# One plain product of two units ahead of the first token sums; three additions for a weight sum, four pieces for a unit's finish

## The chip, the core and the metric

The kernel runs on one core of a Trainium2 chip. The metric is the device time of one execution in microseconds. The kernel was run three times: 2572.38 to 2576.52 us, median 2574.26 us. A separate, profiled execution left the trace from which all rows below are taken.

## The reference, cut to what matters

One decoder layer over 512 tokens of width 2048, batch 1, all in float32. What the change touches is the input projection, one matrix product whose columns are cut into heads, values and gates:

```python
mod = jnp.einsum('bd,de->be', jax.nn.silu(c), w_ada) + b_ada
shift, scale, gate = jnp.split(mod, 3, axis=-1)
u = rms_norm(x, norm_w) * (1.0 + scale[:, None]) + shift[:, None]
proj = jnp.einsum('bsd,de->bse', u, w_in)
(a_q, a_k, a_v, a_z, b_q, b_k, b_v, b_z,
 c_q, c_k, c_v, c_z, g_a, g_b, g_c) = jnp.split(proj, offsets, axis=-1)
...                       # three token mixers, SiLU gates, merge
y = jnp.einsum('bsd,de->bse', merged, w_out)
return x + gate[:, None] * y
```

`c_v`, the values of the dilated mixture, is 3072 columns wide: three of the units below.

## The kernel before, in words

**Precision.** Every float32 operand is split into a rounded high part and a remainder (`uh`, `ul` for the tokens; `xh`, `xl` for weights in this stage; `fh`, `fl` for sums of tokens), and one product takes three matmuls (`mm3`). For weights, ACT writes the high part (`xh`, a CAST of 128x2048) and DVE the remainder (`xl`, a subtraction of the same size): `x_split`.

**Units and jobs.** The stage here runs in the trace from about 221.75 us to about 1290 us. It multiplies 14 blocks of 1024 columns of `w_in` ("units") by a seven-product scheme on 2x2 blocks of tokens and weights. In the text u0, u1 and u2 are the three units of `c_v`; they are the first of the stage. A unit is a list of 14 jobs, each 24 matmuls of 128x512 (48 of 128x256 in the gate and query/key units):
- `P1` (2 jobs) and `P2` (2 jobs): plain products of a block of `u` with a block of weights (`pure_load`, `pure_mul`);
- `R3` (2 jobs): a plain block of weights times the token sum "2";
- 8 sum jobs: each loads four weight blocks, adds them up in place (`sum_load`) and feeds four products, `R6`, `R5`, `R7`, `Q4` (`sum_mul`).

P1, R3 end in `keep` (ACT copies the sum out of PSUM to the tiles `p1`, `r3`), P2 in `p2_done` (DVE adds `p1` to P2, tile `c`). The sum jobs end in `done_z` (DVE takes R6 out of PSUM, tile `z`), `done_s` (R5, tile `s`, then `r3 + s`) and `done_rest` (R7 twice, then Q4).

**PSUM.** There are two rotating groups of banks: `pj` with two, `at` with six. R6 always takes `pj`; R5, R7 and Q4 fill `at`. A product that takes a bank again waits until the engine that empties it has read it.

**The loop over jobs.** Its program order is the order on each engine. For job i: build a token sum if one is due; load job i+2 (with the additions of a sum job on DVE); split job i+1; split the token sum; multiply job i; then one finishing piece that is due, or all that are due when the job just done was the last of a plain product. The split weights have two buffers, so `xh` of job i+2 waits until PE has ended job i. The raw weights `xr` have three.

**Token sums.** `form_build` makes the eight sums of tokens that R3 and the sum jobs need: four DVE subtractions of 128x256 into a tile `d`, from rows of `u` that are read back from DRAM (`xr<-ud`, two DMAs on SP's queue, for every even build). They take a buffer of `xr` as weights do. `form_split` makes `fh` (ACT) and `fl` (DVE) of them. Builds take place in two of every three of the first 12 jobs: `form_build(i - i // 3) if i < 12 and i % 3 < 2`.

**Order of the first units.** `jobs = units[1][0] + units[2][0] + units[0][0] + units[0][1] + units[1][1] + units[2][1]`: P1 and P2 of u1, of u2 and of u0 come first (12 jobs), then R3 and sums of u0, of u1, of u2. For u1 and u2, `p1` waits in DRAM (`p1d`) until its unit's sums begin. From the fourth unit on, a unit runs P1, P2, R3, sums in one go.

Of the kernel before, what the change touches and what calls it, by code (L numbers as in the profile page):

```python
# [10 lines left out]
F32 = mybir.dt.float32  # L11
# [7 lines left out]
P = 128  # L19
# [8 lines left out]
A_Q, A_K, A_V, A_Z = 0, 1024, 2048, 3072  # L28
B_Q, B_K, B_V, B_Z = 4096, 4608, 5120, 6144
# [36 lines left out]
def hybrid_kernel(ctx, tc, x, c, w_in, w_pa, w_pb, w_pc, w_out, w_ada, b_ada, norm_w, lam,  # L66
                  da_w, ret_w, fin_w, k_ident, k_causal, k_band, k_tri4, k_sel, k_cos, k_sin,
                  k_decay, out):
    nc = tc.nc
# [30 lines left out]
    def pj():  # L100
        return psum.tile([P, 512], F32, tag="pj", name="pj", bufs=2)

    def at():
        return psum.tile([P, 512], F32, tag="at", name="at", bufs=6)
# [3 lines left out]
    graw_dram = dram.tile([KC, P, S], F32, tag="graw", name="graw")  # L108

    gate_of = {g: dram.tile([KC, P, S], F32, tag=f"g{g}", name=f"g{g}") for g in (G_A, G_B)}  # L110
    p1_dram = {u: dram.tile([P, 2, 512], F32, tag=f"p1d{u}", name=f"p1d{u}") for u in (3, 4)}
    part_dram = dram.tile([KC, P, S], F32, tag="part", name="part")
    u_dram = dram.tile([KC, P, S], F32, tag="ud", name="ud")

# [420 lines left out]
    def block_mul(pss, name, j, h, l, fm):  # L535

        if fm:
            b = tokens(name, j, slice(0, 256))
            for cb in range(4):
                cs = slice(cb * P, (cb + 1) * P)  # L540
                o = pss[cb // 2][:, (cb % 2) * 256:(cb % 2) * 256 + 256]
                mm3(o, h[:, cs], l[:, cs], *b, j == 0 and cb % 2 == 0, j == HJ - 1 and cb % 2 == 1)
        else:
            for q in range(2):
                mm3(pss[q], *tokens(name, j, slice(q * P, (q + 1) * P)), h, l, j == 0, j == HJ - 1)

    def unit_jobs(w, c0, put, fm=False, early=None):


        st = {}  # L550

        def pure_load(k0, cc):
            r = wxp.tile([P, 4, 512], F32, tag="xr", name="xr", bufs=3)
            sync.dma_start(out=r, in_=w[k0:k0 + 512, cc:cc + 512].rearrange("(j p) c -> p j c", p=P))
            return r

        def pure_mul(key, name, t, hl):
            if t == 0:
                st[key] = [pj() if key == "P1" or (early is not None and key == "R3") else at() for _ in range(2)]
            for jj in range(4):  # L560
                block_mul(st[key], name, 4 * t + jj, hl[0][:, jj, :], hl[1][:, jj, :], fm)

        def keep(key, tag):
            t = evp.tile([P, 2, 512], F32, tag=tag, name=tag)
            for q in range(2):
                act.copy(t[:, q, :], st[key][q])
            st[tag] = t

        def p2_done():
            t = evp.tile([P, 2, 512], F32, tag="c", name="c")  # L570
            for q in range(2):
                dve.tensor_add(t[:, q, :], st["p1"][:, q, :], st["P2"][q])
            put(t, 0, 0)
            if early is not None:
                nc.gpsimd.dma_start(out=early, in_=st["p1"])

        def sum_load(j):
            r = wxp.tile([P, 4, 512], F32, tag="xr", name="xr", bufs=3)
            for i in range(2):
                sync.dma_start(out=r[:, 2 * i:2 * i + 2, :],  # L580
                                     in_=w[(i * HJ + j) * P:(i * HJ + j + 1) * P, c0:c0 + 1024]
                                     .rearrange("p (a c) -> p a c", a=2))
            for o, a in ((0, 1), (1, 3), (3, 0), (2, 3)):
                dve.tensor_add(r[:, o, :], r[:, o, :], r[:, a, :])
            return r

        def sum_mul(j, hl):
            if j == 0:
                st["R6"] = [pj() for _ in range(2)]
                for key in ("R5", "R7", "Q4"):  # L590
                    st[key] = [at() for _ in range(2)]
                if early is not None:
                    st["p1"] = evp.tile([P, 2, 512], F32, tag="p1", name="p1")
                    nc.gpsimd.dma_start(out=st["p1"], in_=early)
            for key, name, o in (("R6", "1", 3), ("R5", "0", 0), ("R7", "3", 1), ("Q4", "A22", 2)):
                block_mul(st[key], name, j, hl[0][:, o, :], hl[1][:, o, :], fm)


        def done_z():
            z = st["z"] = evp.tile([P, 2, 512], F32, tag="z", name="z")  # L600
            for q in range(2):
                dve.tensor_sub(z[:, q, :], st["R6"][q], st["p1"][:, q, :])

        def done_s():
            z, r3 = st["z"], st["r3"]
            s = st["s"] = evp.tile([P, 2, 512], F32, tag="s", name="s")
            for q in range(2):
                dve.tensor_add(s[:, q, :], z[:, q, :], st["R5"][q])
            dve.tensor_add(r3, r3, s)
            put(r3, 0, 512)  # L610

        def done_rest():
            z, s = st["z"], st["s"]
            for q in range(2):
                dve.tensor_add(z[:, q, :], z[:, q, :], st["R7"][q])
                dve.tensor_add(s[:, q, :], s[:, q, :], st["R7"][q])
            put(s, 1, 512)
            for q in range(2):
                dve.tensor_sub(z[:, q, :], st["Q4"][q], z[:, q, :])
            put(z, 1, 0)  # L620

        lists = []
        for key, name, k0, cc, done in (("P1", "A11", 0, 0, lambda: keep("P1", "p1")),
                                        ("P2", "A12", 1024, 0, p2_done),
                                        ("R3", "2", 1024, 512, lambda: keep("R3", "r3"))):
            lists.append([(lambda k0=k0, cc=cc, t=t: pure_load(k0 + t * 512, c0 + cc),
                           lambda hl, key=key, name=name, t=t: pure_mul(key, name, t, hl),
                           (done,) if t == HJ // 4 - 1 else ()) for t in range(HJ // 4)])
        lists.append([(lambda j=j: sum_load(j), lambda hl, j=j: sum_mul(j, hl),
                       (done_z, done_s, done_rest) if j == HJ - 1 else ()) for j in range(HJ)])  # L630
        return lists[0] + lists[1], lists[2] + lists[3]

    def put_values(unit):
        def put(t, half, cc):
            nc.gpsimd.dma_start(out=v_dram[unit][half * 256:half * 256 + 256, cc:cc + 512]
                                .rearrange("(q p) c -> p q c", p=P), in_=t)
        return put
# [4 lines left out]
    def put_gates(g, b0):  # L642
        def put(t, half, cc):
            def f():
                act.activation(out=t, in_=t, func=AF.Sigmoid)
                b = b0 + cc // P
                nc.gpsimd.dma_start(out=gate_of[g][b:b + 4, :, half * 256:half * 256 + 256]
                                    .rearrange("b p t -> p b t"), in_=t.rearrange("p q (a t) -> p (q a) t", a=2))
            deferred.append(f)
        return put  # L650
# [19 lines left out]
    def bias_add(n):  # L670
# [11 lines left out]
        if q == 7:  # L682
            nc.gpsimd.dma_start(out=br_dram[3 * g:3 * g + 3].rearrange("b p c -> p b c"),
                                in_=br.rearrange("p (b c) -> p b c", c=P))


    units = [unit_jobs(w_in, c0, put_values(unit), early=p1_dram.get(unit))
             for unit, c0 in ((2, C_V), (3, C_V + 1024), (4, C_V + 2048))]
    units += [unit_jobs(w_in, g + b0 * P, put_gates(g, b0), fm=True) for g in (G_A, G_B) for b0 in (0, 8)]
    units += [unit_jobs(w_in, c0, put_raw(dst), fm=True) for c0, dst in zip(QK, qk_dram)]  # L690
    units += [unit_jobs(w_in, c0, put_values(unit)) for unit, c0 in ((0, A_V), (1, B_V))]
    jobs = units[1][0] + units[2][0] + units[0][0] + units[0][1] + units[1][1] + units[2][1]
    for plain, summed in units[3:]:
        jobs += plain + summed
    raws = [jobs[0][0](), jobs[1][0]()]
    ready = x_split(raws.pop(0))
    for n, b in enumerate([NF - 1] + list(range(NF - 1))):
# [5 lines left out]
    later = []  # L703
    for i, (_, mul, done) in enumerate(jobs):

        sums = form_build(i - i // 3) if i < 12 and i % 3 < 2 else None
        due, deferred[:] = list(deferred), []
        if i + 2 < len(jobs):
            raws.append(jobs[i + 2][0]())
        nxt = x_split(raws.pop(0)) if raws else None  # L710
        if sums:
            form_split(*sums)
        for f in due:
            f()
        mul(ready)
        ready = nxt
        later += done
        for _ in range(len(later) if len(done) == 1 else min(1, len(later))):
            later.pop(0)()

        u, t = divmod(i, 14)
        if 4 <= u < 12 and t in (6, 8, 10):
            bias_load((u - 4) * 3 + (t - 6) // 2, ("z", "s", "c")[(t - 6) // 2])
        if 4 <= u < 12 and t in (8, 10, 12):
            bias_add((u - 4) * 3 + (t - 8) // 2)
# [1046 lines left out]
```

## Time and profile before

| | us |
|---|---|
| median of three runs (lowest, highest) | 2574.26 (2572.38, 2576.52) |
| the profiled execution, its own time | 2571.79 |
| span of its trace | 2570.0 |
| the first three units, 221.75 to 467.10 us | 245.35 |
| the other units, 467.10 to about 1290 us | 823 |

The span is what the trace covers; the execution's time is 1.8 us longer. PE is the engine that is busy nearly all the time, so a microsecond counts only where PE stands still, or runs at the lower of its two clock levels. The page of the profile gives busy times over the whole span; the views by stretch and of the single instructions show where PE stands.

### The profile page before, as it was taken

How to read it: one execution, taken by the hardware profiler on the slowest of the kernel's cores; microseconds unless marked ns; L12 is line 12 of the kernel's file. 1: busy time of each engine (PE TensorE's matmuls, PEld its weight loads, DVE VectorE, ACT ScalarE, POOL GpSimd, SP SyncE). 2: the span in 40 equal slices, each digit the busy share in tenths (PEclk: the TensorE clock that was granted, in tenths of full speed). 3: DMA queues.
4: the chain of work that ended last, by engine and by line, in shares of the span. 5: the costliest groups of instructions: out<-in, count | busy, mean ns of one | idle time of the engine just before them, and what ended most of it. 6: DMA issues, size and time to landing. Idle time of an engine off the chain costs nothing. (4 is left out here: it accounts for less than half of the span.)

```text
span 2570.0 us, 36726 instructions
## 1 busy us (share of the span) xinstructions
PE 2516.9 (98%) x14539; PEld 2224.0 (87%) x14539; DVE 1907.0 (74%) x2716; ACT 1134.4 (44%) x1476; POOL 179.9 (7%) x293
## 2 busy tenths in 40 slices
PE   7999999999999999999999999999999999999998
PEld 6787777999999999999887888888888888778888
DVE  7885888778887788877886777347887657786554
ACT  5233433443444333333336666346666436652223
POOL 0000000000000000000000001200000220003100
PEclk9999999999999999999999999999999999999999
DMA  9886765666666666666556555654333673439533
GB/s 346 294 293 233 253 213 213 218 209 212 234 233 228 220 209 231 236 223 231 208 183 198 153 160 146 198 162 118 109 113 107 191 222 98 118 113 297 190 133 113
DMA packets 363953, 504.83 MB, mean 196 GB/s; under 512 B 18850, under 2 KB 237748, under 8 KB 363396
## 3 DMA queue, kind: packets, MB, share of 16 engines
q1 hardware_dynamic: 329732, 401.89, 47.8%
q0 software_dynamic: 27136, 92.13, 10.4%
q10 hardware_dynamic: 6912, 8.46, 0.9%
q8 instruction: 114, 1.87, 0.3%
q14 instruction: 59, 0.48, 0.1%
HBM read 450.37 MB, written 52.04 MB: 195 GB/s over the span
## 5 line engine op out<-in xcount | busy, mean ns | idle before, releaser
L86 ACT CAST xh<-xr 128x2048 fp32r<-128x2048 f32 x196 | 374.3, 1910 | 589.7 <-PE at L86 478.8
L86 DVE TENSOR_TENSOR xl<-xr,xh 128x2048 fp32r<-128x2048 f32 x196 | 448.9, 2290 | 184.9 <-ACT xh L86 183.5
L86 DVE TENSOR_TENSOR wl<-wr,wh 128x1024 fp32r<-128x1024 f32 (+2 forms) x275 | 275.4, 1018 | 186.2 <-ACT wh L86 181.4
L86 PE MATMUL pj<-uh,wl 128*128 128x512 f32 x944 | 368.6, 390 | 3.6 <-DVE wl L86 3.6
L86 PE MATMUL pj<-uh,wh 128*128 128x512 f32 x944 | 371.8, 394 | 0.0
L86 ACT CAST wh<-wr 128x1024 fp32r<-128x1024 f32 (+2 forms) x275 | 239.3, 889 | 294.8 <-PE at L86 137.9
L86 PE MATMUL pj<-ul,wh 128*128 128x512 f32 x944 | 368.5, 390 | 0.0
L86 DVE TENSOR_TENSOR xr<-xr 128x512 f32<-128x512 f32 x448 | 309.3, 690 | 13.8 <-DMA xr<-in_w_in_dram 2.3
L86 PE MATMUL at<-fh,xl 128*128 128x256 f32 x864 | 244.9, 283 | 0.7 <-DVE xl L86 0.7
L86 PE MATMUL at<-fh,xh 128*128 128x256 f32 x864 | 244.5, 283 | 0.0
L86 PE MATMUL at<-fl,xh 128*128 128x256 f32 x864 | 244.5, 283 | 0.0
L86 PEld LDWEIGHTS pj<-uh,wl 128*128 128x128 f32 x944 | 177.7, 188 | 41.7 <-DVE wl L86 4.0
L86 PEld LDWEIGHTS pj<-ul,wh 128*128 128x128 f32 x944 | 177.9, 188 | 35.4
L86 PEld LDWEIGHTS pj<-uh,wh 128*128 128x128 f32 x944 | 177.7, 188 | 35.3
L86 PEld LDWEIGHTS at<-fh,xl 128*128 128x128 f32 x864 | 165.8, 192 | 0.9 <-DVE xl L86 0.9
L86 PEld LDWEIGHTS at<-fh,xh 128*128 128x128 f32 x864 | 165.8, 192 | 0.0
L86 PEld LDWEIGHTS at<-fl,xh 128*128 128x128 f32 x864 | 165.8, 192 | 0.0
L86 PE MATMUL at<-uh,xh 128*128 128x256 f32 x576 | 163.0, 283 | 0.0
L86 PE MATMUL at<-ul,xh 128*128 128x256 f32 x576 | 163.0, 283 | 0.0
L86 PE MATMUL at<-uh,xl 128*128 128x256 f32 x576 | 163.0, 283 | 0.0
L86 PE MATMUL at<-yh,wh 128*128 128x512 f32 x288 | 113.1, 393 | 2.2 <-ACT wh L86 2.2
L86 PE MATMUL at<-yh,wl 128*128 128x512 f32 x288 | 112.8, 391 | 0.1
(387 smaller groups left out, 5595.5 us busy)
## 6 DMA issues: line engine op xcount, KB each, us to landing
xr<-in_w_in_dram SPq DMA_DIRECT2D x224, 512.0 KB, 4.5
xr<-in_w_in_dram SPq DMA_DIRECT2D x84, 1024.0 KB, 4.9
wr<-in_w_in_dram SPq DMA_DIRECT2D x116, 512.0 KB, 4.2
wa<-in_w_ada_dram SPq DMA_DIRECT2D x20, 1024.0 KB, 8.3
wr<-in_w_out_dram SPq DMA_DIRECT2D x32, 512.0 KB, 3.9
wr<-in_w_in_dram SPq DMA_DIRECT2D x32, 448.0 KB, 7.6
wb<-in_w_ada_dram SPq DMA_DIRECT2D x12, 1024.0 KB
bw<-in_w_in_dram SPq DMA_DIRECT2D x24, 384.0 KB, 5.5
```

Source lines behind the costliest of these rows:

```text
L86: return lambda *a, **k: pin(f(*a, **k))
```

## The change

The order of the first 42 jobs changes: P1 of u1, of u2 and of u0 (6 jobs), then u0's R3, P2 and sums, u1's R3, P2 and sums, u2's R3, P2 and sums. In all units R3 now stands ahead of P2. One token sum is built in each of the first eight jobs. P1 of u2 and R3 of u1 now take their PSUM from `at`, R3 of u2 from `pj`. The store of `p1` to DRAM stands in `keep`, its load at R3's first job. A weight sum is one addition of 128x1024 and two of 128x512 in place of four of 128x512. The last piece of the finish (Q4) is a piece of its own.

```diff
-    def unit_jobs(w, c0, put, fm=False, early=None):
+    def unit_jobs(w, c0, put, fm=False, early=None, ahead=0):
...
-                st[key] = [pj() if key == "P1" or (early is not None and key == "R3") else at() for _ in range(2)]
+                st[key] = [pj() if key == ("P1" if early is None or ahead == 0 else "R3") else at()
+                           for _ in range(2)]
+            if t == 0 and key == "R3" and early is not None:
+                st["p1"] = evp.tile([P, 2, 512], F32, tag="p1", name="p1")
+                nc.gpsimd.dma_start(out=st["p1"], in_=early)
...
-            for o, a in ((0, 1), (1, 3), (3, 0), (2, 3)):
+            dve.tensor_add(r[:, 0:2, :], r[:, 0:2, :], r[:, 1:4:2, :])
+            for o, a in ((3, 0), (2, 3)):
                 dve.tensor_add(r[:, o, :], r[:, o, :], r[:, a, :])
...
             put(s, 1, 512)
+
+        def done_last():
+            z = st["z"]
             for q in range(2):
                 dve.tensor_sub(z[:, q, :], st["Q4"][q], z[:, q, :])
             put(z, 1, 0)
...
-                                        ("P2", "A12", 1024, 0, p2_done),
-                                        ("R3", "2", 1024, 512, lambda: keep("R3", "r3"))):
+                                        ("R3", "2", 1024, 512, lambda: keep("R3", "r3")),
+                                        ("P2", "A12", 1024, 0, p2_done)):
...
-                       (done_z, done_s, done_rest) if j == HJ - 1 else ()) for j in range(HJ)])
-        return lists[0] + lists[1], lists[2] + lists[3]
+                       (done_z, done_s, done_rest, done_last) if j == HJ - 1 else ()) for j in range(HJ)])
+        return lists[0], lists[1] + lists[2] + lists[3]
...
-    jobs = units[1][0] + units[2][0] + units[0][0] + units[0][1] + units[1][1] + units[2][1]
-    for plain, summed in units[3:]:
-        jobs += plain + summed
+    units = [unit_jobs(w_in, c0, put, fm=fm, early=p1_dram.get(n), ahead=n - 1)
+             for n, (c0, put, fm) in enumerate(specs)]
+    jobs = [job for n in (1, 2, 0) for job in units[n][0]] + units[0][1]
+    for n, (first, others) in enumerate(units[1:], 1):
+        jobs += others if n in p1_dram else first + others
...
-        sums = form_build(i - i // 3) if i < 12 and i % 3 < 2 else None
+        sums = form_build(i) if i < HJ else None
```

**Where the token sums stand on DVE.** In the first jobs of the stage, before the change, a job without a build follows every two with one. Rows of DVE from the second build on (`d` is a sum being built, `fl` its remainder, `xl` the remainder of a job's weights):

```order
L86 TENSOR_TENSOR d<-xr,d 128x256
L86 TENSOR_TENSOR xl<-xr,xh 128x2048
L86 TENSOR_TENSOR fl_1838<-d,fh_1830 128x1024
L86 TENSOR_TENSOR xl<-xr,xh 128x2048
L86 TENSOR_TENSOR d<-xr 128x256
L86 TENSOR_TENSOR d<-xr,d 128x256
L86 TENSOR_TENSOR d<-xr 128x256
L86 TENSOR_TENSOR d<-xr,d 128x256
L86 TENSOR_TENSOR xl<-xr,xh 128x2048
L86 TENSOR_TENSOR fl_1839<-d,fh_1831 128x1024
L86 TENSOR_TENSOR c<-p_1950,at 128x512 x2
```

The same place after the change:

```order
L86 TENSOR_TENSOR d<-xr,d 128x256
L86 TENSOR_TENSOR xl<-xr,xh 128x2048
L86 TENSOR_TENSOR fl_1838<-d,fh_1830 128x1024
L86 TENSOR_TENSOR d<-xr 128x256
L86 TENSOR_TENSOR d<-xr,d 128x256
L86 TENSOR_TENSOR d<-xr 128x256
L86 TENSOR_TENSOR d<-xr,d 128x256
L86 TENSOR_TENSOR xl<-xr,xh 128x2048
L86 TENSOR_TENSOR fl_1839<-d,fh_1831 128x1024
```

The lone `xl` between two pairs of builds and the additions of P2 (`c`) are gone from the stretch: build follows build, one in each job, eight times.

**PE where u0 ends and u1's R3 begins, before.** The rows are the last matmuls of u0's last sum job (`at<-xh,ul`) and the first of R3; the brackets name the engines whose results a row waits for:

```order
L86 MATMUL at<-xh,ul_137 128x512
L86 MATMUL pj<-xh,fh_1829 128x512 [waits DVE_49,Activation_49]
L86 MATMUL pj<-xl,fh_1829 128x512
L86 MATMUL pj<-xh,fl_1837 128x512
L86 MATMUL pj<-xh,fh_1829 128x512 [waits DVE_49]
```

The same place after:

```order
L86 MATMUL at<-xh,ul_137 128x512
L86 MATMUL at<-xh,fh_1829 128x512 [waits DVE_49,Activation_49]
L86 MATMUL at<-xl,fh_1829 128x512
L86 MATMUL at<-xh,fl_1837 128x512
L86 MATMUL at<-xh,fh_1829 128x512 [waits DVE_49]
```

R3 of u1 now writes banks of `at`. Following the rotation of the six banks, the two that it gets are those that R5 of u0 filled: its wait on DVE is a wait for `s<-z,at`, the piece `done_s` of u0, where before it was one for `z<-pj,p` (`done_z`).

**DVE at that place, before.** From `done_z` of u0 on:

```order
L86 TENSOR_TENSOR z<-pj,p_2258 128x512 [waits PE_49] x2
L86 TENSOR_TENSOR xr<-xr 128x512 [waits DMAHW1_49,DVE_49]
L86 TENSOR_TENSOR xr<-xr 128x512 [waits DMAHW2_49,DVE_49]
L86 TENSOR_TENSOR xr<-xr 128x512 [waits DVE_49] x2
L86 TENSOR_TENSOR xl<-xr,xh 128x2048 [waits DMAHW0_49,Activation_49]
L86 TENSOR_TENSOR s<-z,at 128x512 x2
L86 TENSOR_TENSOR r_2406<-r_2406,s 128x1024 [waits DVE_49]
```

The same place after:

```order
L86 TENSOR_TENSOR z<-pj,p_2116 128x512 [waits PE_49] x2
L86 TENSOR_TENSOR xl<-xr,xh 128x2048 [waits DMAHW4_49,Activation_49]
L86 TENSOR_TENSOR s<-z,at 128x512 x2
L86 TENSOR_TENSOR r_2198<-r_2198,s 128x1024 [waits DVE_49]
L86 TENSOR_TENSOR xl<-xr,xh 128x2048 [waits DMAHW5_49,Activation_49]
L86 TENSOR_TENSOR z<-z,at 128x512
...
L86 TENSOR_TENSOR z<-at,z 128x512 [waits DVE_49] x2
L86 TENSOR_TENSOR xr<-xr 128x1024 [waits DMAHW7_49,DMAHW0_49]
L86 TENSOR_TENSOR xr<-xr 128x512 [waits DVE_49] x2
L86 TENSOR_TENSOR xl<-xr,xh 128x2048 [waits DMAHW6_49,PE_49,Activation_49]
```

In both orders `s` stands behind the `xl` of R3's second job. After the change, the additions of the first weight sum (`xr<-xr`) come two jobs later, behind the rest of the finish and ahead of the `xl` of P2's second job (the last row).

## Rows read from the trace of the kernel before

**Rows 1.** Page of the profile, busy time, share of the span, instructions:

```profile
PE 2516.9 (98%) x14539; PEld 2224.0 (87%) x14539; DVE 1907.0 (74%) x2716; ACT 1134.4 (44%) x1476; POOL 179.9 (7%) x293
```

**Rows 2.** By stretch: length, PE PEld DVE ACT POOL busy, granted clock, DMA share, GB/s:

```profile
221.75:348.65 126.90, 123.31 (x530) 99.76 (x528) 97.42 (x104) 55.69 (x41) 3.43 (x5) 0.99 0.69 243
348.65:407.87 59.22, 56.62 (x242) 46.02 (x240) 51.10 (x54) 20.11 (x12) 2.73 (x4) 0.97 0.61 213
407.87:467.10 59.23, 56.53 (x242) 46.05 (x241) 51.11 (x54) 20.10 (x12) 2.73 (x4) 0.97 0.60 213
467.10:1290.00 822.90, 822.10 (x6471) 805.11 (x6470) 658.73 (x652) 313.89 (x203) 34.43 (x46) 1.00 0.65 224
```

**Rows 3.** What PE waited for, 150 to 600 us: total, times, longest:

```profile
PE pj L86 <- ACT r L86: 4.7, 2, 2.5
PE pj L86 <- DVE xl L86: 3.0, 3, 1.8
PE at L86 <- DVE xl L86: 1.7, 3, 0.8
```

**Rows 4.** PE's timeline (start, length): job 2 begins; second R3 job of u1 begins:

```profile
236.88 0.39 PE L86 MATMUL at<-xh,uh 128*128 128x512 f32 x1
...
354.09 0.39 PE L86 MATMUL pj<-xh,fh 128*128 128x512 f32 x1
```

**Rows 5.** PE's timeline behind R3 of u1, where the sums begin:

```profile
362.19 0.50 PE L86 MATMUL pj<-xh,fh 128*128 128x512 f32 x1 [2.50 <-ACT r L86]
...
364.25 0.63 PE L86 MATMUL at<-xh,fh 128*128 128x512 f32 x1
364.68 0.63 PE L86 MATMUL at<-xl,fh 128*128 128x512 f32 x1
```

**Rows 6.** ACT's and DVE's timelines where u2 ends, PE's last sum job at 467.10:

```profile
467.29 1.91 ACT L86 CAST xh<-xr 128x2048 fp32r<-128x2048 f32 x1 [3.53 <-DVE z L86]
...
469.23 2.29 DVE L86 TENSOR_TENSOR xl<-xr,xh 128x2048 fp32r<-128x2048 f32 x1 [1.94 <-ACT xh L86]
471.44 1.28 DVE L86 TENSOR_TENSOR s<-z,at 128x512 f32<-128x512 f32 x2
472.76 1.23 DVE L86 TENSOR_TENSOR r<-r,s 128x1024 f32<-128x1024 f32 x1
```

**Rows 7.** DVE's timeline behind u0: the finish of R7 and Q4, and weight sums:

```profile
361.18 0.68 DVE L86 TENSOR_TENSOR z<-z,at 128x512 f32<-128x512 f32 x1
...
363.57 1.28 DVE L86 TENSOR_TENSOR z<-at,z 128x512 f32<-128x512 f32 x2
364.77 2.86 DVE L86 TENSOR_TENSOR xr<-xr 128x512 f32<-128x512 f32 x4
```

**Rows 8.** ACT's timeline, `keep` of u1's R3:

```profile
361.55 1.08 ACT L86 COPY r<-pj 128x512 f32<-128x512 f32 x2 [5.30 <-DMA vd<-r]
```

**Rows 9.** DVE's timeline, token sums: end of the second build, fifth and sixth, seventh:

```profile
232.15 0.42 DVE L86 TENSOR_TENSOR d<-xr,d 128x256 f32<-128x256 f32 x1
...
260.93 0.43 DVE L86 TENSOR_TENSOR d<-xr 128x256 f32<-128x256 f32 x1 [3.25 <-DMA xr<-ud]
...
264.60 1.22 DVE L86 TENSOR_TENSOR fl<-d,fh 128x1024 fp32r<-128x1024 f32 x1
...
266.87 0.42 DVE L86 TENSOR_TENSOR d<-xr,d 128x256 f32<-128x256 f32 x1
...
278.12 0.43 DVE L86 TENSOR_TENSOR d<-xr 128x256 f32<-128x256 f32 x1 [1.64 <-DMA xr<-ud]
```

**Rows 10.** SP's queue, loads of token rows that those builds waited for:

```profile
252.78 1.01 SPq L86 DMA_DIRECT2D xr<-ud  x2
...
269.92 0.88 SPq L86 DMA_DIRECT2D xr<-ud  x2
```

**Rows 11.** DMA view, 232 to 241 us: KB each, us to landing:

```profile
xr<-ud SPq DMA_DIRECT2D x2, 512.0 KB, 5.5
```

**Rows 12.** Page of the profile, DMA issues over the span:

```profile
xr<-in_w_in_dram SPq DMA_DIRECT2D x84, 1024.0 KB, 4.9
```

More of the change, by code (lines that the diff above doesn't have):

```diff
@@ L110, in hybrid_kernel @@
     gate_of = {g: dram.tile([KC, P, S], F32, tag=f"g{g}", name=f"g{g}") for g in (G_A, G_B)}
-    p1_dram = {u: dram.tile([P, 2, 512], F32, tag=f"p1d{u}", name=f"p1d{u}") for u in (3, 4)}
+    p1_dram = {u: dram.tile([P, 2, 512], F32, tag=f"p1d{u}", name=f"p1d{u}") for u in (1, 2)}
     part_dram = dram.tile([KC, P, S], F32, tag="part", name="part")
@@ L567, in keep @@
             st[tag] = t
+            if early is not None and tag == "p1":
+                nc.gpsimd.dma_start(out=early, in_=t)
         def p2_done():
@@ L573, in p2_done @@
             put(t, 0, 0)
-            if early is not None:
-                nc.gpsimd.dma_start(out=early, in_=st["p1"])
         def sum_load(j):
@@ L587, in sum_mul @@
         def sum_mul(j, hl):
[L588 to L594, printed above, removed]
             for key, name, o in (("R6", "1", 3), ("R5", "0", 0), ("R7", "3", 1), ("Q4", "A22", 2)):
+                if j == 0:
+                    st[key] = [pj() if key == "R6" else at() for _ in range(2)]
                 block_mul(st[key], name, j, hl[0][:, o, :], hl[1][:, o, :], fm)
@@ L684, in bias_add @@
                                 in_=br.rearrange("p (b c) -> p b c", c=P))
[L687 to L691, printed above, removed]
-    jobs = units[1][0] + units[2][0] + units[0][0] + units[0][1] + units[1][1] + units[2][1]
-    for plain, summed in units[3:]:
-        jobs += plain + summed
+    specs = [(c0, put_values(unit), False) for unit, c0 in ((2, C_V), (3, C_V + 1024), (4, C_V + 2048))]
+    specs += [(g + b0 * P, put_gates(g, b0), True) for g in (G_A, G_B) for b0 in (0, 8)]
+    specs += [(c0, put_raw(dst), True) for c0, dst in zip(QK, qk_dram)]
+    specs += [(c0, put_values(unit), False) for unit, c0 in ((0, A_V), (1, B_V))]
+    units = [unit_jobs(w_in, c0, put, fm=fm, early=p1_dram.get(n), ahead=n - 1)
[3 more added lines that the diff above has]
+        jobs += others if n in p1_dram else first + others
     raws = [jobs[0][0](), jobs[1][0]()]
```

## The prediction

> **What bounds the kernel now.** The page's busy times say PE: 2516.9 of 2570.0 us, 98% [rows 1]. What the change can give or take is therefore only the time in which PE stands still in this stage, or runs at the lower clock. The view by stretch shows where that is. From 467.10 us on, units four and later, PE is busy 822.10 of 822.90 us [rows 2]: nothing is to be gained there. Ahead of it lie three stretches: 126.90 us for the 22 jobs up to u1's R3, then 59.22 and 59.23 us for ten jobs each. One undisturbed job lasts 354.09 - 348.65 = 5.44 us [rows 4] (348.65 is where the second stretch begins [rows 2]). Ten jobs are 54.4 us, so each of the two transitions u0-u1 and u1-u2 loses 4.8 us. Job 2 begins at 236.88 [rows 4], and the 20 jobs up to 348.65 take 111.77 us against 108.8: 3.0 us are lost beside the token sums. What comes before job 2 stays as it is. Together 12.6 us: that is all that a perfect edit could win.
>
> The view of waits names the causes: two waits for ACT's copy of R3, 4.7 us together, and six short ones for `xl` [rows 3]. The timeline shows the price of a stop: after one of 2.50 us the matmuls start 0.43 us apart (364.25, 364.68) instead of 0.227 [rows 5]; the granted clock of these two stretches is 0.97 against 1.00 [rows 2], so some of their matmuls ran at 1.2 instead of 2.4 GHz. The rest of a transition's loss, 4.8 - 2.5 = 2.3 us, is these low-clock matmuls (I take 1.7) and small waits.
>
> **Parts that cost and bring nothing.** The fourth finishing piece: the second job after the sums is the last of a plain product and empties the list, so Q4's piece still runs behind R7's; order unchanged. Three additions for four: a sum took 2.86 us [rows 7]; one of 128x1024 takes 1.23 [rows 6] and two of 128x512 some 1.3, so 2.55, 0.3 less on DVE. From 467 us on DVE waits for PE, not PE for DVE [rows 2], so that 0.3 us is no time; at the two transitions it is inside the sums below. Without that cover each of 112 sums would be worth 0.3 us; PE's 0.8 us of idle time there says that it is not so. After the swap of R3 and P2 in later units, Q4 takes its banks from DVE's two `c` additions (1.3 us, as `s` [rows 6]) instead of ACT's copy; 18 matmuls, 4.1 us, stand between: nothing, and some 1 us for each unit if DVE came 4 us late. The store of `p1` on POOL's queue goes out one plain product earlier; its load, now ahead of the store of `r`, is issued in 0.6 us or so and has ten jobs until its use: nothing.
>
> **The two old stops go.** At both transitions R6's wait for ACT's copy came from `keep` of R3, which itself waited 5.30 us for the store `vd<-r` to land [rows 8], with R6 right behind R3 in the same `pj` banks. P2's two jobs now lie between: 4.8 us at each transition, 9.6 in all, can go.
>
> **What takes their place at u0-u1.** R3 of u1 now writes the banks of R5 and waits for `s` of u0. In DVE's order `s` stands behind the `xl` of R3's second job, this one behind ACT's `xh`, and `xh` needs the buffer that PE frees with its last matmul of u0. The same chain without a waiting PE is at u2's end: PE done at 467.10, `xh` 467.29, `xl` 469.23, `s` 471.44, its first half done at 472.08 [rows 6]. So PE stands 5.0 us, 5.1 with the semaphore. A stop of 2.5 us already brought the slow matmuls [rows 5], so I add 1.7 us. Then P2 takes a bank that ACT's copy of R3 must empty first, and R3's last matmul has just ended: half of 1.08 [rows 8] and its start, about 1.0 with small waits. Behind that DVE is late. After PE's first R3 job (12.2 us from u0's end: 5.1 + 1.7 + 5.4) come `xh` and `xl` (4.2), the finish of R7 and Q4 (361.18 to 364.77, 3.6) [rows 7], a sum (2.55), `xl` of P2's second job (2.3): 24.9. PE reaches the matmul that needs it at 12.2 + 5.4 + 1.0 + 5.4 + 0.2 = 24.2, less what of the low clock falls into the copy. I take 1.6 us, with its clock: the nearer bound, 0.7, and the far one, 2.5, make the range. Sum: 5.1 + 1.7 + 1.0 + 1.6 + 0.4 for small waits = 9.8 against 4.8.
>
> **At u1-u2** R3 stands in `pj` and waits only for `z`, done in time as before. The finish then delays DVE the same way: 5.4 + 4.2 + 3.6 + 2.55 + 2.3 = 18.1 us after u1's end, where PE needs it at 3 x 5.44 + 0.2 = 16.5. PE stops 1.6 to 1.9 us, plus 1.6 at the low clock, plus 0.3: 3.7 against 4.8. Both transitions: 13.5 against 9.6, so **+3.9** (from +2 to +6: without the low clock and the second wait, or with both stops at their far bounds).
>
> **The token sums.** Before, a job without a build followed every two. Now the eight builds run in a row, and each pair needs its rows of `u`, whose load must wait for the pair before, since all take the same third buffer of `xr`. A cycle is: load L, then 260.93 to 267.29 on DVE for two builds with `xl` and `fl` between them [rows 9], 6.4 us. PE needs 10.9 us for two jobs. The second build ends at 232.57 [rows 9]; three cycles and the last `xl` and `fl` (3.35) later, the eighth sum is there at 255.1 + 3L. PE wants it in R3's second job, job 7, at its 21st matmul: 236.88 + 5 x 5.44 + 4.5 = 268.6. So the loss is **3L - 13.5**.
>
> L is the open price. The two loads that DVE waited for took, from issue to the build's start, 260.93 - 252.78 = 8.15 and 278.12 - 269.92 = 8.2 us [rows 9, 10]. The first pair's halves landed in 5.5 us [rows 11], some 6.0 from the first issue. Weight loads of the same megabyte have a median of 4.9 [rows 12]. A weight load goes out when an `xl` has freed its buffer. After the change one such load runs ahead of each of these by `fl` and a build, 2.6 us, and on SP's queue another stands behind it and goes out one `xl`, 2.3 us, later (its own use is over 10 us off, so this queueing costs nothing more). That speaks for 8.2; but fewer stores run beside them. I take 6.0, 7.3, 7.3: 20.6 - 13.5 = 7.1, plus 0.9 of slow matmuls behind the last stop, 8.0 against 3.0: **+5.0** (from -1 at L = 4.9 to +9 at 8.2). It falls mostly as waits for `xl` in jobs 3, 5, 6 and as one for `fl` in job 7.
>
> Here the Trainium skill speaks for the kind end: "DMA: Bandwidth & Descriptors", section on the anatomy of one DMA (SWDGE path), fits a transfer as 2.0 us plus its bytes by 436e3 per us, which would be 4.4 us for a megabyte on a free path. The trace does not agree in this stretch (8.15 us [rows 9, 10]), and by the page's figure, an estimate, the token sums would lose nothing and the whole change would cost about 1 us.
>
> **Sum.** 3.9 + 5.0 = +8.9 us: the profiled execution from 2571.79 to 2580.7, and, by the same difference, the median from 2574.26 to 2583.2 (the profiled execution lies 2.5 us below the median). A difference below 0.2%, 5.1 us, can't be told from none here.
>
> **Rivals.**
> 1. *Loads land as other loads do*, L about 4.9 to 5.5. For it: the first pair, and fewer stores. Against: both waited loads. Token sums -1 to 0, transitions +3.9: **2577**, no difference to be told. Chance 0.22.
> 2. *Every load takes 8.2 us*: 24.6 - 13.5 + 1 - 3.0 = +9.1, with the transitions +13: **2587**. For it: the weight load in front of each. Chance 0.2.
> 3. *Faster*: PE doesn't wait for `s` at u0-u1, because DVE and ACT get through before PE ends u0, as `done_z` did at u2's end; then 9.6 us go at the two transitions with nothing in their place, and the token sums cost 3 to 5: **2569**. It decides at the wait of R3's first matmul: below some 1 us there. Against: `xh` needs PE's last matmul, so the chain can't start earlier. Chance 0.08.
> 4. *The order does nothing*, old stops replaced by equal ones and the token sums covered: 2574 to 2576. Chance 0.05.
>
> The forecast has 0.45. Faster by over 0.2% is 0.08, within 0.2% 0.25 (rival 1, rival 4 and a little of the forecast's low end), slower 0.67. The range for 8 in 10 leaves out rival 3 and the far end of 2: 2575 to 2591.
>
> **What would show it.** In the waits of the changed kernel: PE `at` waiting once for 5 us at R3 of u1, for DVE `s`; no wait for ACT `r` of over 1 us; `xl` waits of 1 to 3 us in jobs 3 to 7; token row loads of 6 to 8 us. The stretches then hold 18, 12 and 12 jobs in place of 22, 10 and 10: job 0 to u1's R3 about 97.9 + 4.3 + 8.0 = 110 us, u1 65.3 + 9.8 = 75, u2 65.3 + 3.7 = 69, and the later units 823 as before. I am wrong if R3 of u1 starts on time, if token rows land in 5 us, or if units after the third change.

## The result, and the profile after

The changed kernel takes 2580.13 us (median of 17 runs, 2576.01 to 2583.82), the kernel before 2573.82 us beside it (17 runs). The ratio is 1.0024, 95% interval 1.0017 to 1.0031: **6.2 us slower**, 4.4 to 8.0. That is inside the range and near the forecast of +8.9. The new trace has a span of 2578.9 us, 8.9 more than the one before; two single executions can differ by some us more or less than the medians do, and here 2.7 of the 8.9 us are such a difference.

The first view is again the one by stretch: the 18 jobs to u1's R3, u1, u2, and the units after them, up to the first job of the last unit on both sides. (In the trace of before that unit begins at 1270.58 us and the stage ends at about 1347 us, not at about 1290.)

```profile
221.04:329.77 108.73, 100.60 (x433) 80.27 (x431) 84.50 (x88) 48.11 (x37) 1.96 (x3) 1.00 0.67 234
329.77:403.94 74.17, 67.86 (x290) 55.08 (x289) 55.94 (x50) 24.02 (x14) 3.46 (x5) 0.98 0.61 206
403.94:471.32 67.38, 65.77 (x290) 53.90 (x288) 56.06 (x50) 23.94 (x14) 3.45 (x5) 1.00 0.66 226
...
471.32:1278.23 806.91, 803.40 (x6386) 789.03 (x6384) 632.57 (x559) 305.02 (x197) 32.27 (x43) 1.00 0.66 222
```

The last of these stretches in the kernel before:

```profile
467.10:1270.58 803.48, 802.68 (x6385) 789.00 (x6384) 644.70 (x639) 305.17 (x197) 32.26 (x43) 1.00 0.64 222
```

The first three answer to [rows 2], whose stretches hold 22, 10 and 10 jobs; the new ones hold 18, 12 and 12. Set against 5.44 us for each job, the first two of the new ones lose 3.6 and 4.1 us more than before and the third 2.7 us less. The units behind lose 3.4 us that were not forecast, in u4 to u7 (counted from u0; the expectations call them units four to seven). What PE waited for in 150 to 600 us, beside [rows 3]:

```profile
PE at L86 <- DVE xl L86: 8.0, 6, 1.7
PE at L86 <- DVE s L86: 5.0, 1, 5.0
PE pj L86 <- DVE xl L86: 3.2, 2, 1.8
PE at L86 <- DVE fl L86: 1.3, 1, 1.3
```

ACT's copy of R3 is gone from the list: the two old stops went, as the change could have it. In their place stand one wait of 5.0 us for `s`, and many for `xl`.

The chain at u0's end, where PE is done at 329.77: ACT, DVE, then PE's first matmuls of R3, with their starts 0.43 us apart.

```profile
329.97 1.90 ACT L86 CAST xh<-xr 128x2048 fp32r<-128x2048 f32 x1 [3.53 <-DVE z L86]
...
331.90 2.29 DVE L86 TENSOR_TENSOR xl<-xr,xh 128x2048 fp32r<-128x2048 f32 x1 [1.93 <-ACT xh L86]
334.11 1.28 DVE L86 TENSOR_TENSOR s<-z,at 128x512 f32<-128x512 f32 x2
...
334.94 0.77 PE L86 MATMUL at<-xh,fh 128*128 128x512 f32 x1 [5.00 <-DVE s L86]
335.50 0.63 PE L86 MATMUL at<-xl,fh 128*128 128x512 f32 x1
335.93 0.63 PE L86 MATMUL at<-xh,fl 128*128 128x512 f32 x1
```

It is [rows 6] again, moved to a place where PE stands behind it. PE's other stops up to the third unit, from its timeline:

```profile
242.19 0.50 PE L86 MATMUL at<-xl,uh 128*128 128x512 f32 x1 [1.68 <-DVE xl L86]
...
254.76 0.50 PE L86 MATMUL pj<-xl,uh 128*128 128x512 f32 x1 [1.39 <-DVE xl L86]
...
266.76 0.50 PE L86 MATMUL at<-xl,fh 128*128 128x512 f32 x1 [0.83 <-DVE xl L86]
...
272.70 0.50 PE L86 MATMUL at<-xh,fl 128*128 128x512 f32 x1 [1.29 <-DVE fl L86]
...
280.64 0.50 PE L86 MATMUL at<-xl,uh 128*128 128x512 f32 x1 [1.06 <-DVE xl L86]
...
354.87 0.50 PE L86 MATMUL at<-xl,uh 128*128 128x512 f32 x1 [1.31 <-DVE xl L86]
...
422.25 0.50 PE L86 MATMUL at<-xl,uh 128*128 128x512 f32 x1 [1.61 <-DVE xl L86]
```

The first four are the token sums, in jobs 3, 5, 7 and again 7; the fifth is a wait of another kind (below); the last two are P2's second job in u1 and u2, behind the finish. SP's issues of the token rows, and DVE where it waits for them, show L (beside [rows 9, 10]):

```profile
231.90 0.88 SPq L86 DMA_DIRECT2D xr<-ud  x2
...
244.76 0.88 SPq L86 DMA_DIRECT2D xr<-ud  x2
...
257.33 0.88 SPq L86 DMA_DIRECT2D xr<-ud  x2
...
238.38 0.43 DVE L86 TENSOR_TENSOR d<-xr 128x256 f32<-128x256 f32 x1 [3.17 <-DMA xr<-ud]
...
250.94 0.43 DVE L86 TENSOR_TENSOR d<-xr 128x256 f32<-128x256 f32 x1 [2.60 <-DMA xr<-ud]
...
262.95 0.42 DVE L86 TENSOR_TENSOR d<-xr 128x256 f32<-128x256 f32 x1 [2.31 <-DMA xr<-ud]
...
275.70 2.68 DVE L86 TENSOR_TENSOR xr<-xr 128x1024 f32<-128x1024 f32 x3 [3.05 <-DMA xr<-in_w_in_dram]
```

L was 6.48, 6.18 and 5.62 us. The last row is the first weight sum: its load takes the buffer that the eighth token sum has just freed, and the `xl` of job 9 stands behind its additions.

### The profile page after: what moved, and what is told of

The parts are those of the page before. It is cut to its first block, busy times and chain, and to the rows that moved or that the text cites. A ratio compares the mean times of both kernels' runs of the same rounds, so it can differ in the third digit from the quotient of the medians.

```text
span 2578.9 us, 36570 instructions
## 1 busy us (share of the span) xinstructions
PE 2516.4 (98%) x14539; PEld 2221.8 (86%) x14539; DVE 1891.4 (73%) x2604; ACT 1134.3 (44%) x1476; POOL 179.0 (7%) x293
## 5 line engine op out<-in xcount | busy, mean ns | idle before, releaser
L86 DVE TENSOR_TENSOR xr<-xr 128x1024 f32<-128x1024 f32 x336 | 291.8, 868 | 45.0 <-DMA xr<-in_w_in_dram 36.8
L86 PEld LDWEIGHTS at<-uh,xl 128*128 128x128 f32 x576 | 110.6, 192 | 4.3 <-DVE xl L86 4.3
```

Of the source, the lines that this page charges most:

```text
L86: return lambda *a, **k: pin(f(*a, **k))
```

## The experiments

Each ran in five rounds beside the kernel before; a ratio is to the kernel before, with its 95% interval. How much faster a run is than the changed kernel is the difference of the two ratios, times 2574 us; with both intervals it is good to about 3 us.

**1. R3 of u1 back in pj.**

```diff
-                st[key] = [pj() if key == ("P1" if early is None or ahead == 0 else "R3") else at()
+                first = early is None or ahead == 0
+                st[key] = [pj() if (key == "P1" and first) or (key == "R3" and early is not None) else at()
                            for _ in range(2)]
```

> The changed kernel with one thing undone: R3 of u1 takes its PSUM from pj again. Theory (the stop at u1 comes from R5's banks, so from done_s): PE's 5.0 us wait for s is gone and with it the low clock behind it, and u1's stretch looks like u2's: 74.2 us becomes 67 to 68, the kernel 6 to 7 us faster than the changed one, about level with the one before. Rival (DVE and ACT are late at that place whatever the bank, so the stop moves to P2 or to R6): the stretch stays at 72 to 74 us and the time within 2 us of the changed kernel.

Measured: 2572.16 us, ratio 0.9998 (0.9989 to 1.0007), 6.7 us faster than the changed kernel. u1's stretch:

```profile
330.19:398.07 67.88, 66.12 (x290) 53.83 (x288) 55.78 (x50) 23.94 (x14) 3.46 (x5) 1.00 0.66 225
```

Within the expected 67 to 68, at a granted clock of 1.00 in place of 0.98, and `s` is no longer among the waits of PE. The theory holds: the whole net loss of the change is as large as this one choice of a bank.

**2. Four additions again, in the changed kernel.**

```diff
-            dve.tensor_add(r[:, 0:2, :], r[:, 0:2, :], r[:, 1:4:2, :])
-            for o, a in ((3, 0), (2, 3)):
+            for o, a in ((0, 1), (1, 3), (3, 0), (2, 3)):
```

> The changed kernel with the four additions of 128x512 for a weight sum back. Theory (the one addition of 128x1024 reads both halves of the load, so it can't begin on the first half while the second is under way; this is the 3.4 us lost in the units after the third): units four to seven lose 1 us or less together, the kernel 2 to 3.4 us faster than the changed one, although DVE does 0.2 us more work in each of 112 sums. Rival (the order of R3 and P2 lost that time): units after the third stay at 806 to 807 us, and the two transitions get 0.2 us longer each.

Measured: 2580.48 us, ratio 1.0029 (1.0018 to 1.0039): no gain. The trace says otherwise of u4 to u7: the waits for `xl` there are 2.0 us in all against 3.5 of the changed kernel (1 us or less was expected). In u4 DVE begins when the first half has landed, and goes on when the second has:

```profile
577.42 0.69 DVE L86 TENSOR_TENSOR xr<-xr 128x512 f32<-128x512 f32 x1 [1.59 <-DMA xr<-in_w_in_dram]
...
579.95 1.42 DVE L86 TENSOR_TENSOR xr<-xr 128x512 f32<-128x512 f32 x2 [1.84 <-DMA xr<-in_w_in_dram]
```

The unit begins at 554.20, so the halves are there at 23.2 and 25.75 us. In the changed kernel the unit begins at 551.95, and the one addition over both starts at 25.76 us (577.71). The mechanism is as stated; its worth is not, in the time. The granted clock can account for the difference: over a whole execution it was 0.9946 in the mean of this kernel's seven and 0.9956 in that of the changed kernel's 17. A thousandth of 2580 us is 2.6 us (an estimate from these numbers), as much as u4 to u7 could have gained. Why the clock was lower is not shown.

**3. Three additions, in the kernel before.** The reverse of the edit of 2.

> The kernel before with one thing of the change alone: three additions for a weight sum. Theory (the addition over both halves waits for the later one): 1.5 to 3.5 us slower than the kernel before, all of it between units four and seven. Rival (less work on DVE helps the two transitions and hurts nowhere, the loss comes from R3 ahead of P2): 0 to 1 us faster than the kernel before.

Measured: 2572.82 us, ratio 0.9996 (0.9987 to 1.0005). Not 1.5 us slower; at most 1.3. Its trace shows the loss in u4 to u7 all the same, 3.4 us of waits against 0.7, and its span is 2.7 us longer than that of before; the medians are not. By the estimate of 2, 1.5 us of what is missing lie in the granted clock, 0.9961 in the mean here and 0.9955 in the kernel before. Neither theory nor rival as written: the three additions lose time in a place that can be pointed at, and the whole kernel does not show it.

**4. Token rows loaded one pair ahead**, the second and fourth load into the tiles `c` and `r3`.

```diff
+    def form_load(j):
+        r = wxp.tile([P, 4, 512], F32, tag="xr", name="xr", bufs=3)
+        if j % 4:
+            form_rows[j // 2] = [evp.tile([P, 2, 512], F32, tag=t, name="fr") for t in ("c", "r3")]
+        else:
+            form_rows[j // 2] = [r[:, 0:2, :], r[:, 2:4, :]]
...
             raws.append(jobs[i + 2][0]())
+        if i % 2 == 0 and i + 2 < HJ:
+            form_issue(i + 2)
```

> The changed kernel with the rows of u for the token sums loaded one pair ahead: the second and fourth load go to the tiles c and r3, which are free then, so no load waits for the build before it. Theory (3L - 13.5: the builds wait for loads, each of which must wait for the pair before): the DVE waits for rows of u vanish, jobs 2 to 17 take 88 us or little more against 93.6, and the kernel is 4 to 6 us faster than the changed one. Rival (one build in each job is too much for DVE and ACT, or the queue holds the weight loads back): PE still waits for xl in these jobs, and the gain is under 2 us.

Measured: 2574.67 us, ratio 1.0004 (0.9995 to 1.0013), 5.1 us faster than the changed kernel. The 18 jobs:

```profile
222.26:324.89 102.63, 99.61 (x433) 80.52 (x431) 84.69 (x88) 47.96 (x37) 1.97 (x3) 1.00 0.73 248
```

102.63 us against 108.73, and no `d` waits for rows of `u`. Jobs 2 to 17 take 89 us against 95.1 (the 93.6 of the expectation was too low). One build in each job is a small burden for DVE and ACT when the rows are there, with stops of 0.2 and 1.0 us left in PE: most of the loss was the load.

**5. Both together** (1 and 4).

> The changed kernel with the two repairs together: R3 of u1 in pj, and rows of u loaded one pair ahead. Theory (two separate losses, in stretches that don't touch): the gains add up, 6.7 and 5.2 us, some 12 us faster than the changed kernel and 4 to 7 us faster than the kernel before (ratio 0.9975 to 0.9985). Rival (the one gain only moves a wait into the other place): no more than 8 us faster than the changed kernel, level with the one before.

Measured: 2567.66 us, ratio 0.9976 (0.9967 to 0.9985): 6.2 us faster than the kernel before, 12.4 faster than the changed one; the two gains alone make 11.8. They add up.

**6. Both, with four additions.**

> The kernel with both repairs, and four additions of 128x512 for a weight sum. Theory, after two runs in which the times did not bear out the profiles: three additions or four makes less than 2 us, and which is faster can't be told. Rival (the addition over both halves holds up units four to seven): 2 to 3 us faster than the kernel with both repairs and three additions. Second rival (0.3 us less on DVE in each of 112 sums is worth something at the transitions): 1 us slower.

Measured: 2567.91 us, ratio 0.9979 (0.9970 to 0.9987). Not to be told from the three additions, as expected.

**7. Both, with the finishing pieces really taken one per job.** In the changed kernel the end of a plain product still empties the list.

```diff
-        later += done
-        for _ in range(len(later) if len(done) == 1 else min(1, len(later))):
-            later.pop(0)()
+        if len(done) == 1:
+            done[0]()
+        else:
+            later += done
+        if later:
+            later.pop(0)()
```

> The kernel with both repairs, and the finishing pieces really taken one per job: when a plain product ends only its own copy or addition runs, and the piece for Q4 waits for the next job. Theory (the stop of 1.3 to 1.6 us at P2's second job is DVE late by the finish ahead of a weight sum): Q4's 1.2 us leave the way of that xl, each of the two stops falls to 0.4 us or less, and the kernel is 1.5 to 3 us faster than with both repairs alone. Rival (the stop is the load of the first weight sum, or a later piece finds its buffer taken): no gain, or a new wait of 1 us at P2 or R5.

Measured: 2562.80 us, ratio 0.9958 (0.9946 to 0.9970), the fastest of all: 10.8 us under the kernel before. The stops at P2's second job fell to 0.41 us, but two of 0.25 us came up behind each, so u1 and u2 gained only 0.2 and 0.3 us (67.39 and 67.07 against 67.56 and 67.38). The larger part of the 4.6 us came from u4 to u7, where no wait is left: a place that the expectation did not name.

**8. Both, with R3 behind P2 again in the later units.**

```diff
+        if not early and not lead:
+            return lists[0], lists[2] + lists[1] + lists[3]
         return lists[0], lists[1] + lists[2] + lists[3]
```

> The kernel with both repairs, and R3 behind P2 again in the eleven units after the third. Theory (in those units the order of R3 and P2 costs nothing, as forecast): within 1.5 us of the kernel with both repairs, and PE waits for xl in units four to seven as much as there. Rival (R3 ahead of P2 is what lost 3 us there): 2 to 3 us faster, with only one wait left in unit four.

Measured: 2567.83 us, ratio 0.9976 (0.9967 to 0.9986), the same as with the swap, and its trace has three waits for `xl` of 3.3 us in all after the third unit. The order of R3 and P2 costs nothing there.

**9. The spread finish alone, in the changed kernel** (the edit of 7).

> The changed kernel with nothing but the finishing pieces really taken one per job. Theory (the 3 to 4 us lost in units four to seven come from Q4's piece and its Sigmoid standing ahead of the third job's weights, whose buffer the first weight sum's load waits for): PE's waits for xl after the third unit vanish, these units take 803 us again, the stop of 5.0 us for s and the token sums stay as they are, and the kernel is 3.5 to 5.5 us faster than the changed one (ratio to before 1.0003 to 1.0012). Rival (the gain in the repaired kernel came from the first units, where a freed microsecond can be kept): less than 2 us.

Measured: 2576.01 us, ratio 1.0008 (0.9999 to 1.0017), 4.1 us faster than the changed kernel, and the profile has no wait of PE after the third unit; the stretch from u3 to the last unit is back at 802.7 us. The size is as expected, but the reason given was wrong. The buffer that the first weight sum's load waits for comes free at the same time, 16.4 us into u4 (the end of the third job's `xl`, 568.38 and 570.56). Rows of DVE and POOL, first the changed kernel (unit from 551.95):

```profile
566.09 2.29 DVE L86 TENSOR_TENSOR xl<-xr,xh 128x2048 fp32r<-128x2048 f32 x1 [0.47 <-ACT xh L86]
...
577.71 2.68 DVE L86 TENSOR_TENSOR xr<-xr 128x1024 f32<-128x1024 f32 x3 [4.13 <-DMA xr<-in_w_in_dram]
...
567.31 0.75 POOL L650 DMA_DIRECT2D g<-s  x1 [5.61 <-ACT s L86]
568.25 0.75 POOL L650 DMA_DIRECT2D g<-z  x1 [0.19 <-issue]
```

Then the spread finish (unit from 554.13):

```profile
568.27 2.29 DVE L86 TENSOR_TENSOR xl<-xr,xh 128x2048 fp32r<-128x2048 f32 x1 [1.67 <-ACT xh L86]
...
578.30 2.67 DVE L86 TENSOR_TENSOR xr<-xr 128x1024 f32<-128x1024 f32 x3 [2.53 <-DMA xr<-in_w_in_dram]
...
569.49 0.75 POOL L650 DMA_DIRECT2D g<-s  x1 [5.61 <-ACT s L86]
574.70 0.75 POOL L650 DMA_DIRECT2D g<-z  x1 [4.45 <-ACT z L86]
```

What differs is the store of `z`. In the changed kernel it goes out 0.9 us behind that of `s`, at the moment at which the load is issued, and load and store run together: the load's data are there 9.3 us after the buffer came free. With the store 4.3 us later it is 7.7 us. The DMA view of the twelve us from 566 and 568.2 on agrees: the store of `z` took 8.9 and then 4.8 us, a half of a weight load 7.5 and then 6.5 (medians). That the store delays the load is read from these rows; no run moved the store alone.

**10. Experiment 7 with four additions.**

> Both repairs and the spread finish, with four additions of 128x512. Theory (three additions lose only where a load lands last, and no load does there any more): the three additions' 0.2 to 0.3 us show without their cost, 0.5 to 1.5 us slower than with three. Rival (waiting for both halves costs in many jobs, not only in those where PE is seen to wait): 1 to 3 us faster.

Measured: 2565.90 us, ratio 0.9964 (0.9950 to 0.9977), 1.5 us slower than with three, which the intervals can't tell from none. In its trace the stops are 0.60, 0.44 and 0.45 us where three additions have 0.41, 0.25 and 0.25.

## Why the prediction was right, step by step

**The old stops go, and R3 of u1 waits for `s`: right.** 5.00 us were measured for 5.1 forecast, behind the chain that was named, and experiment 1 takes away all of it. u1 lost 74.17 - 65.28 = 8.9 us against 9.8 forecast. The terms: the stop as said; the low clock cost some 1.6 us (seven matmuls start 0.43 us apart or more, and then one 0.30), 1.7 forecast; the second stop was 1.31 us, 1.6 forecast; the copy of R3 delayed P2 by some 0.3 us, not the 1.0 set for it. The rest, 0.7 us where 0.4 were set, is in slower first matmuls behind the stops and small waits.

**u1-u2: right in the mechanism, mis-sized.** The stop of 1.61 us is there (1.6 to 1.9 forecast). The term "1.6 at the low clock" measured nothing: the granted clock of u2's stretch is 1.00 and the matmuls behind the stop start 0.23 to 0.24 us apart. So u2 lost 2.1 us, not 3.7. Together the transitions lost 11.0 us where 9.6 were lost before: +1.4, not +3.9; the low end of the range given was +2.

**The token sums: right in the mechanism; the term L was set too high, and two smaller things made up for it.** With the L that was measured, the chain 231.87 (end of the second build) + 18.28 + 3 x 6.4 + 3.35 gives 272.7 us for the eighth `fl`; DVE ended it at 272.65. But the loads took 18.3 us together, not 20.6. Two things were left out: the first weight sum's load waits for the eighth token sum's buffer, 1.06 us of PE; and PE came to job 2 1.5 us earlier than before, since its first matmuls ran at the full clock this time, so it waited that much longer. Jobs 2 to 17 lost 329.77 - 234.68 - 87.04 = 8.05 us, 8.0 forecast, by chance so close. By the fit in the Trainium skill ("DMA: Bandwidth & Descriptors", anatomy of one DMA, which is for the SWDGE path) a megabyte would take 4.4 us, an estimate. The trace does not agree: it shows 1.2 to 2.1 us more, on SP's queue and with other transfers on the way. The rival "loads land as other loads do" had the better L for the last load alone (5.62); it fell on the stretch, which lost 8 us and not 2 to 3.

**"From 467 us on ... nothing": wrong in the trace, by 3.4 us.** The prediction named a change in these units as a sign that it is wrong. The step that failed is "that 0.3 us is no time": DVE's sum was costed by its length, not by what it waits for. (The length was off too: three additions took 2.68 us against 2.86, 0.2 less and not 0.3.) One addition over both halves can't start until the later one has landed (experiment 2 shows the rows). The six traces with three additions and the old finish lost 3.4 to 4.7 us in u4 to u7 over four times 80.65 us, the three with four additions and the old finish 1.0 to 2.5. Between kernels that differ in nothing else, three additions cost 1.8 to 3.3 us there. With the finish spread the loss is 0.5 us or less in all three traces, with three additions or four (experiments 7, 9 and 10). So in the traces the loss needs the finish in one go, and the three additions make it larger. The medians don't bear out the part of the additions: 2 against the changed kernel, 3 against before, 6 against 5 and 10 against 7 all lie within 1.5 us, each with three additions ahead, and the granted clock can explain this for 2, and in part for 3. What the three additions are worth over the whole kernel stays open, within about 3 us to either side. What the medians do show is the finish (experiment 9, 4.1 us); they show no cost of the swap of R3 and P2 (experiment 8).

**"The fourth finishing piece ... order unchanged": right**, and it is where the change left something lying: with the piece really set apart, the kernel gains 4 us (experiments 7 and 9).

So the sign, the two causes and their places were right. In the trace the terms are 1.4 for the transitions, 5.1 for the token sums, -1.5 for jobs 0 and 1 at the full clock, and 3.4 for the later units: 8.4, and 0.5 more ahead of the stage (-0.7) and behind the last of the stretches (+1.2). The forecast of 8.9 came out so near because errors of both signs met, the transitions 2.5 us too dear and the later units forgotten: its nearness is luck. The medians are only 6.2 us apart, so 2.7 us of the difference belong to the two single executions; in which of the terms they lie is not known.

## What to carry to other kernels

When the order of work changes, follow the rotation of the PSUM banks to the name of the result that frees each one: the same R3 in another pair of banks was worth 6.7 us, because the instruction that freed it stood, in DVE's order, behind work that could start only when PE was done. A buffer shared between two kinds of load ties the one to the other's end; a chain of "load, use, load" that was hidden with a free job in each three showed its full length once the free job was gone, and two idle tiles broke it for 5.1 us. Where a merged instruction reads two transfers it waits for the later one, so cost it by its inputs' arrival and not by its length.

## What was not expected of the hardware

The same stop is not always followed by matmuls at the lower clock. At PE's first job of the stage every trace has a stop of 1.82 or 1.83 us. Its stretch before the change (the view by stretch, job 0 to 15 us), and after it:

```profile
221.75:236.80 15.05, 13.20 (x49) 9.92 (x48) 10.36 (x14) 7.42 (x8) 0.00 (x0) 0.89 0.72 261
```

```profile
221.04:234.60 13.56, 11.70 (x49) 8.80 (x48) 9.74 (x14) 7.42 (x8) 0.00 (x0) 1.00 0.68 242
```

The work is the same (49 matmuls, 14 instructions of DVE, 8 of ACT). The granted clock is 0.89 in the one and 1.00 in the other, that is, some matmuls at 1.2 GHz or all at 2.4, and the difference is 1.5 us. With experiment 5 it was 0.89 and 15.14 us again, in a kernel with the changed order; of the twelve traces eight have the lower clock behind this stop and four don't. At u2's P2 a stop of 1.61 us left 1.00 in the changed kernel, and one of 1.79 us was followed by 0.83 over ten us in experiment 2, with some 1.6 us lost; behind those of 1.79 and 1.80 us in experiment 6 it stayed at 1.00. So a stop of this length has no fixed price. The Trainium skill ("TensorE: Matmul & The Clock Gate", Part 1) says of the start of a kernel that the count of slow matmuls varies between runs of one kernel. The traces agree, and for stops inside a kernel too (the eight and the four above). The stops of 5.0 us were followed by the lower clock in each of the four traces that have one, with matmuls 0.43 us apart.
